# The last two eighths of the second feed-forward matrix taken together, and filler matmuls in planned gaps of TensorE

## The chip, the core and the metric

The kernel runs on one core of a Trainium2 chip. The metric is the device time of one execution in microseconds (us). TensorE (PE) multiplies matrices; VectorE (DVE), ScalarE (ACT) and GpSimd (POOL) do the elementwise work; SyncE (SP) issues the DMAs. TensorE's clock has two levels in this profile: a granted share of 1.0 is 2.4 GHz, of 0.5 is 1.2 GHz.

## What is computed

Two trunk layers run over 640 tokens: 128 prompt tokens and 512 sample tokens, which share all weights. From the reference, cut to the part that matters here:

```python
def trunk_layer(h, mod, lp, init, pos):
    sh1, sc1, g1, sh2, sc2, g2 = jnp.split(mod, 6, axis=-1)
    y, states = mixing_block(layer_norm(h) * (1.0 + sc1) + sh1, lp, init, pos)
    h = layer_norm(DEEPNORM_ALPHA * h + g1 * y, lp['ln1_g'], lp['ln1_b'])
    u = layer_norm(h) * (1.0 + sc2) + sh2
    f = jnp.square(jax.nn.relu(u @ lp['w_ff1'])) @ lp['w_ff2']
    h = layer_norm(DEEPNORM_ALPHA * h + g2 * f, lp['ln2_g'], lp['ln2_b'])
    return h, states
```

The model width is 1024, the hidden width of the feed-forward part 4096. `mixing_block` holds an input projection, four recurrent mixers (mLSTM, gated DeltaNet, retention, RWKV-7), and an output projection `w_out`.

## The kernel before, in words

**Tiles.** The 640 tokens are five tiles of 128: the group GA = tiles 0, 1, 2 and the group GB = tiles 3, 4. Matmuls run in fp32r on pairs: each operand is split into a high part (`wh`, `uh`, `hid` high) and a low rest (`wl`, `ul`), and a product is three matmuls. A weight block of 512 KB is loaded by SP into `wr`, cast by ACT (sometimes DVE) into `wh`, and the rest `wl` is formed by POOL or DVE (`split`). There are three `wr` buffers and two each of `wh` and `wl`. Six more buffers of the pool `pnz` are shared: they hold the hidden activations of an eighth, and some weights that are split early ("spare").

**Stages of a layer.** First the mixers: input projections (`pj`), scans, inverses (`lv`), head outputs (`pt` transposes of `osum`). Then `w_out` (`pwo`) and its layer norms (`wout_mm`, `wout_ln`), transposition into features for the feed-forward part (`put`, tiles `v`), and the feed-forward part in eighths of 512 hidden columns, counted by `hb`: `ff1(hb)` makes `hid` (four weight blocks, matmuls into `pj`), `ff2(hb)` multiplies with rows of `w_ff2` into banks `pff`, for two column halves of 512. Eighths 0 to 6 do `ff2` for all five tiles, four blocks of 30 matmuls, and add into `acc` (`add_first`, `add_mid`). Eighth 7 does `ff2` for GA first, four blocks of 18 matmuls, and then for GB, four blocks of 12, with `add_last`: scale by the gate (`fft`) and add to `acc`. Before that, `acc` is scaled and the residual `xr` is added to it. `final_ln` follows for GA beside the matmuls of GB, and then for GB; in layer 0 the result is normed once more and transposed (`put`) into the features `uh`, `ul` of layer 1, GA's 24 transposes first, then GB's 16.

**The modulation of layer 1** (`mod_chunk_v`, twelve chunks of four weight blocks, on ACT, DVE and POOL with a short `pmt` product on PE) is spread over layer 0's eighths: `next_mods(MB[0])` beside `ff1`, `next_mods(MB[1])` beside `ff2`.

**What sets the order.** Nothing is issued as it is written. Every operation is recorded as a node, and `Plan.schedule` runs a list scheduler over all of them: it has a cost for each instruction, a priority from the code's order and the longest path, room in the buffer pools, and a model of TensorE's clock (`hist`, `recent`, `cols`: matmul columns of the last few us). Its result is one fixed order for each engine, and each engine executes its own in that order. All instructions come out of one line (`emit`), so the profile names them all L743; they are told apart by their tiles.

## Time and profile before

| | |
|---|---|
| time of three runs | 2376.15 us median (2375.57 to 2382.08) |
| time of the profiled execution | 2374.3 us |
| its span, first to last instruction | 2372.5 us |
| mean granted TensorE clock | 0.939 |
| busy share | PE 89%, DVE 65%, ACT 40%, POOL 33% |

A row of the page's first part gives an engine's busy time, its share of the span and its instructions. PEclk in the second part is the granted clock in tenths, over 40 equal slices of the span. A matmul's record overlaps the next, so a mean duration is longer than the time from one start to the next. A matmul of plain f32 leaves two records.

### The profile page before, as it was taken

How to read it: one execution, taken by the hardware profiler on the slowest of the kernel's cores; microseconds unless marked ns; L12 is line 12 of the kernel's file. 1: busy time of each engine (PE TensorE's matmuls, PEld its weight loads, DVE VectorE, ACT ScalarE, POOL GpSimd, SP SyncE). 2: the span in 40 equal slices, each digit the busy share in tenths (PEclk: the TensorE clock that was granted, in tenths of full speed). 3: DMA queues.
4: the chain of work that ended last, by engine and by line, in shares of the span. 5: the costliest groups of instructions: out<-in, count | busy, mean ns of one | idle time of the engine just before them, and what ended most of it. 6: DMA issues, size and time to landing. Idle time of an engine off the chain costs nothing.

```text
span 2372.5 us, 42057 instructions
## 1 busy us (share of the span) xinstructions
PE 2113.5 (89%) x16510; PEld 1850.1 (78%) x16510; DVE 1544.2 (65%) x3245; ACT 949.9 (40%) x2018; POOL 774.0 (33%) x696
## 2 busy tenths in 40 slices
PE   5999989898786999999969989799897699999996
PEld 2887768787666888888947888689786589999995
DVE  5577767686679566667695768578785933333357
ACT  3444243343245544444344453343341443333332
POOL 2241323433246343335372325225361710000023
PEclk8999999999797999999977999899898899999998
DMA  8132442636343444444531222314353412222242
GB/s 265 28 73 73 112 101 74 171 91 176 127 139 118 141 134 134 134 133 138 158 116 37 64 43 69 71 54 99 91 149 129 141 61 72 80 72 80 72 160 89
DMA packets 317450, 253.12 MB, mean 107 GB/s; under 512 B 91100, under 2 KB 240828, under 8 KB 317252
## 3 DMA queue, kind: packets, MB, share of 16 engines
q1 hardware_dynamic: 317252, 250.43, 36.6%
q8 instruction: 130, 2.13, 0.4%
q14 instruction: 68, 0.56, 0.1%
HBM read 226.14 MB, written 24.24 MB: 106 GB/s over the span
## 4 chain that ended last, share of the span: by engine, by line
PE 57%; DVE 19%; DMA 9%; POOL 5%; issue 4%; ACT 3%; SPq 2%; DVEq 0%; POOLq 0%; ACTq 0%
PE pj L743 25%; PE pff L743 17%; DMA wr<-in_w_mod 3%; PE pwo L743 2%; SPq L743 2%; PE lv L743 2%; PE poo L743 2%; DVE xn L743 2%; DMA wr<-in_w_in 2%; DVE osum L743 1%; DVE lnrs L743 1%; DVE lnst L743 1%; DMA gh<-wscr 1%; DVE etmp L743 1%; DVE acc L743 1%
## 5 line engine op out<-in xcount | busy, mean ns | idle before, releaser
L743 ACT CAST wh<-wr 128x1024 fp32r<-128x1024 f32 x231 | 241.9, 1048 | 512.7 <-PE pff L743 225.0
L743 PE MATMUL pff<-wh,hid 128*128 128x512 f32 x1280 | 398.1, 393 | 0.0
L743 POOL TENSOR_TENSOR wl<-wr,wh 128x1024 fp32r<-128x1024 f32 x90 | 221.9, 2468 | 367.0 <-ACT wh L743 340.6
L743 DVE TENSOR_TENSOR wl<-wr,wh 128x1024 fp32r<-128x1024 f32 x144 | 188.8, 1311 | 214.0 <-ACT wh L743 213.7
L743 PE MATMUL pj<-uh,wl 128*128 128x256 f32 (+1 forms) x1056 | 309.3, 335 | 3.5 <-POOL wl L743 3.5
L743 PE MATMUL pj<-ul,wh 128*128 128x256 f32 (+1 forms) x1056 | 309.1, 335 | 0.0
L743 PE MATMUL pj<-uh,wh 128*128 128x384 f32 (+1 forms) x1056 | 306.1, 334 | 2.8 <-DVE dec L743 1.4
L743 PE MATMUL pj<-vh,wl 128*128 128x384 f32 (+1 forms) x1024 | 287.9, 312 | 1.8 <-POOL wl L743 1.1
L743 PE MATMUL pj<-vh,wh 128*128 128x384 f32 (+1 forms) x1024 | 285.3, 313 | 2.8 <-ACT wh L743 2.7
L743 PE MATMUL pj<-vl,wh 128*128 128x384 f32 (+1 forms) x1024 | 284.7, 312 | 0.0
L743 PEld LDWEIGHTS pff<-wh,hid 128*128 128x128 f32 x1280 | 239.7, 189 | 51.5 <-ACT wh L743 0.2
L743 PE MATMUL pff<-wl,hid 128*128 128x512 f32 x640 | 245.9, 397 | 10.3 <-POOL wl L743 10.0
L743 PEld LDWEIGHTS pj<-uh,wl 128*128 128x128 f32 x1056 | 193.4, 195 | 20.8 <-issue 9.5
L743 PEld LDWEIGHTS pj<-uh,wh 128*128 128x128 f32 x1056 | 193.2, 196 | 18.3 <-issue 7.0
L743 PEld LDWEIGHTS pj<-ul,wh 128*128 128x128 f32 x1056 | 194.2, 196 | 13.3 <-issue 8.7
L743 PEld LDWEIGHTS pj<-vh,wh 128*128 128x128 f32 x1024 | 186.5, 190 | 8.4 <-ACT wh L743 4.2
L743 PEld LDWEIGHTS pj<-vh,wl 128*128 128x128 f32 x1024 | 185.6, 190 | 4.7 <-POOL wl L743 1.5
L743 PEld LDWEIGHTS pj<-vl,wh 128*128 128x128 f32 x1024 | 186.0, 190 | 2.6 <-issue 1.4
L743 POOL TENSOR_TENSOR mac<-mac,mtm 128x512 f32<-128x512 f32 x77 | 114.1, 1482 | 177.4 <-ACT mtm L743 167.2
L743 DVE TENSOR_TENSOR hid<-sqr,hid 128x256 fp32r<-128x256 f32 (+1 forms) x125 | 73.0, 586 | 136.9 <-ACT hid L743 136.3
L743 POOL TENSOR_TENSOR acc<-acc,bc 128x512 f32<-128x512 f32 x16 | 26.8, 1693 | 387.8 <-DMA xr<-x1d 363.4
L743 PEld LDWEIGHTS pff<-wl,hid 128*128 128x128 f32 x640 | 119.2, 189 | 35.9 <-POOL wl L743 12.6
(499 smaller groups left out, 4139.8 us busy)
## 6 DMA issues: line engine op xcount, KB each, us to landing
wr<-in_w_ff SPq DMA_DIRECT2D x136, 512.0 KB
wr<-in_w_mod SPq DMA_DIRECT2D x96, 512.0 KB
wr<-in_w_in SPq DMA_DIRECT2D x66, 512.0 KB
wr<-in_w_out SPq DMA_DIRECT2D x32, 512.0 KB
dq<-rscr SPq DMA_DIRECT2D x20, 256.0 KB
dec<-rscr SPq DMA_DIRECT2D x16, 320.0 KB
x1d<-x SPq DMA_DIRECT2D x20, 256.0 KB
xr<-x1d SPq DMA_DIRECT2D x20, 256.0 KB
```

What stands on the lines that cost most here:

```text
L743: fn(*[res(v) for v in a], **{k_: res(v) for k_, v in k.items()})
```

## The change

It does four things.

1. `ff2` for eighth 6 is no longer done apart. `ff1(6)` and `ff1(7)` run in a row, and `ff2` then takes both at once, eight blocks of 18 matmuls for GA and then eight of 12 for GB. The hidden activations of eighth 6 stand in eight slots of the general pool.
2. Spare buffers take the early weights of three projections (`SPA = (6, 7, 8)`) and not of one.
3. Layer 1's modulation takes 6 and 2 steps in each of six eighths, before 5 and 2 in each of seven.
4. Stretches of the code are marked as zones (`thin`, `zone`): from the features `y` through `w_out` to the features `v`, and from GB's `ff2` through the final norm to the next layer's features, in both layers, and the first features at the start. Where the planner has no ready matmul for PE inside a zone, and its count of recent columns is under 1.3 of its mark, it puts in a filler: a 128x128 f32 matmul of the identity with 128 columns of constants into a fresh PSUM bank `warm`, which nothing reads.

Its core:

```diff
-    MB = (5,2,0,0,0,0)
-    SPA = (6,)
+    MB = (6,2,0,0,0,0)
+    SPA = (6, 7, 8)
...
+        FT, FT0, FB, FN = 1.3, 12.0, 2, 128
...
+                        if e == "PE" and (q is None or q is early) and now > FT0 and recent - part < FT * 3100 and any(a <= floor < b for a, b in self.zones) and caps[self.bank] > FB:
+                            nd, x = filler(now)
+                            d = nd.dur + (SW if nd.mode != mode else 0.0)
...
+    plan.warm = lambda n: (ident, cst[:, 0:n])
+    plan.warm_fn = lambda *a: nc.tensor.matmul(*a, start=True, stop=True)
...
-                hd = pnz.tile([128, 2, TOK], F32R, tag="nz", name=f"hid_{uid[0]}")
-                hi, lo = hd[:, 0, :], hd[:, 1, :]
+                if hb == 6:
+                    hi, lo = slot(TOK, "hid", F32R), slot(TOK, "hid", F32R)
+                else:
+                    hd = pnz.tile([128, 2, TOK], F32R, tag="nz", name=f"hid_{uid[0]}")
+                    hi, lo = hd[:, 0, :], hd[:, 1, :]
...
-                yield from acts_mm(hh, hl, tiles, (0, 1), lambda kk: I["w_ff2"][l, 512 * hb + 256 * kk:512 * hb + 256 * kk + 256, 512 * h_:512 * h_ + 512], banks)
+                yield from acts_mm(hh, hl, tiles, range(len(hid) // 2), lambda kk: I["w_ff2"][l, 512 * hb + 256 * kk:512 * hb + 256 * kk + 256, 512 * h_:512 * h_ + 512], banks)
...
-        for hb in range(7):
+        for hb in range(6):
...
+        run((ff1(6, hid), 8, "f"))
         run((ff1(7, hid), 8, "f"))
...
-        run((ff2(7, hid, GA, add_last), 6))
-        run((final_ln(GA), 3), (ff2(7, hid, GB, add_last), 6), (next_mods(MB[2]), 4))
+        run((ff2(6, hid, GA, add_last), 6))
+        with thin():
+            run((final_ln(GA), 3), (ff2(6, hid, GB, add_last), 6), (next_mods(MB[2]), 4))
```

The multiplications are the same, 240 `pff` matmuls for the two eighths of a layer. The weight blocks of eighth 6 are now loaded and split twice, once for GA and once for GB: four blocks more in each layer, 80 DMAs of 128x2x512 where there were 72. Ten `add_mid` per layer fall away. There are 163 fillers: 2 at the start; in layer 0, 17 ahead of `pwo` and 38 from the last `pwo` into the feed-forward part; 25 at the boundary of the layers; in layer 1, 16 ahead of `pwo` and 32 after it; and in the last stage 9 among the matmuls and 24 behind the last one.

Since the planner runs over everything at once, the order moves elsewhere too. With buffer numbers left out and set side by side, 8230 of some 12,900 PE instructions keep their place relative to each other, and the mixers of both layers are among what moved.

At the boundary of the layers, PE's queue before has GB's last matmuls and behind them the transposes of GA (`xn` are normed rows, `pff` banks of GB):

```order
L743 MATMUL pff_12618<-wh_12625,hid_12345 128x512
L743 MATMUL pff_12608<-wh_12625,hid_12416 128x512
L743 MATMUL pff_12618<-wh_12625,hid_12416 128x512
L743 MATMUL pff_12618<-wl_12650,hid_12416 128x512
L743 MATMUL pff_12618<-wh_12625,hid_12416 128x512
L743 MATMUL put_12710<-cst,xn_12702 128x128
L743 MATMUL put_12712<-cst,xn_12702 128x128
```

In the change, the first transposes stand inside GB's matmuls, behind 52 of the 96:

```order
L810 MATMUL warm_12760<-cst 128x128
L810 MATMUL warm_12764<-cst 128x128
L775 MATMUL pff_12704<-wl_12734,hid_11829 128x512
L775 MATMUL pff_12715<-wl_12734,hid_11829 128x512
L775 MATMUL put_12776<-cst,xn_12748 128x128
L775 MATMUL pff_12704<-wh_12699,hid_11838 128x512
L775 MATMUL pff_12715<-wh_12699,hid_11838 128x512
L775 MATMUL put_12786<-cst,xn_12748 128x128
L775 MATMUL pff_12704<-wh_12699,hid_11904 128x512
```

So `put` was behind all of GB's matmuls, and now 44 of them are queued behind the first `put`; 34 stand behind the eighth, and 11 behind the ninth. Between GA's transposes and GB's first, PE has 47 matmuls of the next projections (`pj`, `pgj`) before and 81 in the change.

In layer 1, ahead of the bulk of `pwo`, PE's queue before is this (`pt` transposes the last head output, `yh` is a feature of it after a trip through HBM):

```order
L743 MATMUL poo_19827<-Rd_18948,dec_17952 128x64
L743 MATMUL pt_3315_19867<-cst,osum_19720 128x128
L743 MATMUL pt_3316_19869<-cst,osum_19720 128x128 x4
L743 MATMUL pwo_19199<-wh_19490,yh_19881 128x512
L743 MATMUL pwo_19199<-wl_19559,yh_19881 128x512
```

and in the change:

```order
L775 MATMUL pt_3321_20039<-cst,osum_19920 128x128
L775 MATMUL pt_3322_20041<-cst,osum_19920 128x128 x4
L810 MATMUL warm_20051<-cst 128x128
L810 MATMUL warm_20053<-cst 128x128
L810 MATMUL warm_20055<-cst 128x128
```

16 fillers follow the five transposes there, all ahead of the first `pwo` that needs the last head.

## Rows read from the trace of the kernel before

**Rows 1.** The page's first and second part: busy time, granted clock by slice.

```profile
PE 2113.5 (89%) x16510; PEld 1850.1 (78%) x16510; DVE 1544.2 (65%) x3245; ACT 949.9 (40%) x2018; POOL 774.0 (33%) x696
PEclk8999999999797999999977999899898899999998
```

**Rows 2.** Busy time by stage, with its column line: mixers, feed-forward, boundary, end.

```profile
core 0: us, PE busy (x) PEld busy (x) DVE busy (x) ACT busy (x) POOL busy (x), PEclk, DMA share, GB/s
55.00:640.00 585.00, 534.81 (x5427) 462.55 (x5426) 414.80 (x1128) 227.46 (x584) 195.61 (x191) 0.94 0.39 103
754.00:1174.00 420.00, 411.97 (x2467) 370.49 (x2466) 270.01 (x298) 203.69 (x350) 154.79 (x97) 1.00 0.46 140
1196.00:1256.00 60.00, 34.73 (x144) 27.13 (x143) 53.51 (x87) 27.28 (x56) 45.38 (x47) 0.69 0.35 107
1256.00:1802.00 546.00, 496.92 (x5173) 445.23 (x5171) 394.16 (x1097) 218.31 (x563) 204.11 (x203) 0.94 0.32 80
1911.00:2316.00 405.00, 405.00 (x2299) 370.33 (x2299) 151.01 (x194) 146.11 (x251) 14.72 (x10) 1.00 0.27 85
2339.00:2373.00 34.00, 11.05 (x38) 7.65 (x36) 29.35 (x43) 6.77 (x8) 20.00 (x19) 0.73 0.21 77
```

**Rows 3.** PE's timeline at the boundary: start, duration, operation, [idle before, releaser].

```profile
1198.58 0.50 PE L743 MATMUL pff<-wl,hid 128*128 128x512 f32 x1 [0.45 <-POOL wl L743]
1209.18 0.80 PE L743 MATMUL pff<-wl,hid 128*128 128x512 f32 x1 [3.59 <-POOL wl L743]
1216.47 1.11 PE L743 MATMUL put<-cst,xn 128*128 128x128 f32 x4 [2.65 <-ACT xn L743]
1231.88 3.03 PE L743 MATMUL put<-cst,xn 128*128 128x128 f32 x13 [7.47 <-ACT xn L743]
1242.76 0.33 PE L743 MATMUL pj<-ul,wh 128*128 128x384 f32 x1
1242.93 0.33 PE L743 MATMUL pj<-uh,wl 128*128 128x384 f32 x1
1245.38 0.48 PE L743 MATMUL put<-cst,xn 128*128 128x128 f32 x1 [2.12 <-ACT xn L743]
```

**Rows 4.** PE's timeline, GB's part of the last eighth in layer 1.

```profile
2335.77 0.39 PE L743 MATMUL pff<-wh,hid 128*128 128x512 f32 x1
2336.00 0.39 PE L743 MATMUL pff<-wl,hid 128*128 128x512 f32 x1
2338.98 0.85 PE L743 MATMUL pff<-wh,hid 128*128 128x512 f32 x3
2340.28 0.50 PE L743 MATMUL pff<-wl,hid 128*128 128x512 f32 x1 [0.45 <-POOL wl L743]
2344.25 0.51 PE L743 MATMUL pff<-wl,hid 128*128 128x512 f32 x1 [0.95 <-POOL wl L743]
2350.94 0.55 PE L743 MATMUL pff<-wl,hid 128*128 128x512 f32 x1 [3.64 <-POOL wl L743]
2354.69 0.40 PE L743 MATMUL pff<-wh,hid 128*128 128x512 f32 x1
```

**Rows 5.** DVE's timeline at the end: the last bank's evacuation.

```profile
2358.53 0.68 DVE L743 TENSOR_TENSOR fft<-pff,bc 128x512 f32<-128x512 f32 x1
```

**Rows 6.** Groups by line: the two ways to form `wl`.

```profile
L743 POOL TENSOR_TENSOR wl<-wr,wh 128x1024 fp32r<-128x1024 f32 x90 | 221.9, 2468 | 367.0 <-ACT wh L743 340.6
L743 DVE TENSOR_TENSOR wl<-wr,wh 128x1024 fp32r<-128x1024 f32 x144 | 188.8, 1311 | 214.0 <-ACT wh L743 213.7
```

**Rows 7.** Nine stretches at the low clock inside the zones, summed by the same view as rows 2.

```profile
sum 122.80, PE 55.17 PEld 44.99 DVE 86.35 ACT 45.67 POOL 71.62; mean PE 6.13 PEld 5.00 DVE 9.59 ACT 5.07 POOL 7.96
```

**Rows 8.** Low stretches in which PE works without a break: two of `pwo`, then the sum of seven.

```profile
655.30:658.20 2.90, 2.83 (x7) 2.09 (x8) 0.84 (x2) 0.00 (x0) 0.00 (x0) 0.50 0.15 55
1817.30:1822.20 4.90, 4.84 (x11) 3.65 (x12) 0.83 (x2) 0.59 (x1) 0.00 (x0) 0.50 0.07 25
sum 23.20, PE 23.08 PEld 19.78 DVE 14.92 ACT 12.70 POOL 10.46; mean PE 3.30 PEld 2.83 DVE 2.13 ACT 1.81 POOL 1.49
```

**Rows 9.** PE's timeline around the gaps ahead of `pwo`, and a plain f32 matmul by form.

```profile
655.37 0.79 PE L743 MATMUL pwo<-wh,yh 128*128 128x512 f32 x1 [6.27 <-DVE yh L743]
1817.36 0.80 PE L743 MATMUL pwo<-wh,yh 128*128 128x512 f32 x1 [6.40 <-DVE yh L743]
L743 PE MATMUL pqs<-Yd,cvo 128*128 128x128 f32 x64 | 13.0, 302 | 0.2 <-DVE dtm L743 0.2
```

More of the change, by code (lines that the diff above doesn't have):

```diff
@@ L215, in __init__ @@
     def __init__(self):
-        self.nodes, self.tiles = [], []
+        self.nodes, self.tiles, self.zones = [], [], []
         self.HY = 1.0
@@ L484, in schedule @@
         HM = 1.2
+        FT, FT0, FB, FN = 1.3, 12.0, 2, 128
+        self.nfill = 0
         HG = 1.0
@@ L556, in schedule, with filler @@
         RES = 1
+        def filler(now):
+            x = self.warm_tile().tile
+            caps[x.key] -= 1
+            x.seq = x.at = x.end_seq = floor
+            load[x.key][floor] += 1
+            x.alloc = True
+            nd = Node()
+            nd.eng, nd.nm, nd.idx, nd.tiles, nd.preds, nd.succs, nd.grp = "PE", "matmul", len(N) + len(out), [x], [], [], None
+            nd.a, nd.k, nd.fn = (x.view()[:, 0:FN],) + self.warm(FN), {}, self.warm_fn
+            nd.mem, nd.act, nd.mode = [("matmul", nd.fn, nd.a, nd.k)], self.activity("matmul", nd.a[0], nd.a), self.pe_mode(nd.a)
+            nd.dur = self.pe_time(nd.mem)
+            return nd, x
         def eligible(nd, t):
@@ L826, in bankB, with thin, warm_tile @@
         return psA.tile([128, 512], F32, tag="a", name=f"{name}_{uid[0]}")
+    @contextmanager
+    def thin():
+        a = len(plan.nodes)
+        yield
+        plan.zones.append((a, len(plan.nodes)))
+    def warm_tile():
+        uid[0] += 1
+        return psA.tile([128, 512], F32, tag="a", name=f"warm_{uid[0]}")
+    plan.warm_tile = warm_tile
+    plan.bank = (id(psA), "a")
     def mm(out, lhsT, rhs, start=True, stop=True):
@@ L1431, in hybrid_step @@
     dma(out=mskt, in_=I["masks"])
-    run((to_features(0, 0, xn0, feats, FGA + FGB), 24))
+    with thin():
+        run((to_features(0, 0, xn0, feats, FGA + FGB), 24))
     for l in range(layers):
@@ L2272, in hybrid_step @@
         run((n3, 30), (ret_scan(1, C_[1], R_), 20, "f"), (mod_some(40), 40))
+        zone = len(plan.nodes)
         yhl = new_features("y")
@@ L2312, in hybrid_step @@
         run((wout_mm(GA), 10))
-        run((wout_ln(GA), 3), (wout_mm(GB), 10))
-        u2 = new_features("v")
-        run((to_features(l, 2, xn, u2, FGA), 16))
-        if l + 1 < layers:
-            load_params(l + 1)
-            nmod = mod_gen(l + 1, (0, 2, 1, 3) + tuple(range(4, NMX)))
-        run((wout_ln(GB), 2))
-        run((to_features(l, 2, xn, u2, FGB), 8))
+        plan.zones.append((zone, len(plan.nodes)))
+        with thin():
+            run((wout_ln(GA), 3), (wout_mm(GB), 10))
+            u2 = new_features("v")
+            run((to_features(l, 2, xn, u2, FGA), 16))
+            if l + 1 < layers:
+                load_params(l + 1)
+                nmod = mod_gen(l + 1, (0, 2, 1, 3) + tuple(range(4, NMX)))
+            run((wout_ln(GB), 2))
+            run((to_features(l, 2, xn, u2, FGB), 8))
         u2h, u2l = [f[0] for f in u2], [f[1] for f in u2]
```

31 lines of the change are left out of this document (23 added, 8 removed).

## The prediction

> **What bounds the kernel now.** I read the page's busy shares and clock first, then busy time by stage, then PE's timeline where PE stands still. PE is busy 89% of the span, no other engine over 65%, and PEclk dips in some slices [rows 1]. The stages differ [rows 2]. The feed-forward part of layer 1 is PE alone: 405.0 of 405 us. In layer 0 the same part has 8.0 us of PE idle in 420, beside the modulation of the next layer. The mixers leave PE idle for 50.2 us of 585 in layer 0 and 49.1 of 546 in layer 1. At the boundary of the layers, 1196 to 1256, PE works 34.7 of 60 us while DVE works 53.5, at a mean clock of 0.69: there the norms on DVE set the pace, and PE waits for `xn` with 2.65 us, 7.47 us and later 2.12 us of idle ahead of transposes [rows 3]. In the last 34 us DVE works 29.4 and PE 11.1 [rows 2]. So PE work that moves into the boundary is hidden, and a shorter stay at the low clock pays only where PE has work queued.
>
> **Part 1: eighth 6 joins eighth 7.** Matmuls of `pff` start 0.23 us apart at full clock [rows 4]. GB's 48 matmuls of eighth 6 (48 x 0.23 = 11.0 us) leave the place ahead of GA's end, where PE is busy without a break, and join GB's own 48 behind it.
>
> At the boundary they fall into 60 - 34.7 = 25.3 us of PE idle. GA's end comes 11.0 us earlier, and the DVE-bound stretch behind it stays as long as it was, but for four more weight blocks. One costs DVE 1.31 us or POOL 2.47 us [rows 6]; all on DVE would be 5.2 us, all on POOL 9.9 us of the 14.6 us that POOL is idle there [rows 2], or none. I take +4 (0 to +10), near the DVE price, since DVE has only 6.5 us free. The ten `add_mid` that fall away lay beside PE's work in eighth 6, so I count nothing for them. The spare buffers let 81 projection matmuls stand ahead of GB's transposes and not 47; they start 0.17 us apart [rows 3], so up to 34 x 0.17 = 5.8 us of work moves into the idle stretch that begins at 1243. What moves must wait for its weights, and those come when the hidden tiles are freed, so I take -3 (0 to -5.8). Sum at the boundary: -11.0 + 4 - 3 = **-10** (-16.8 to -1).
>
> At the kernel's end there is no next layer to hide in. Before, the stretch from 2339.0 to the end is 33.5 us, and 11.0 us of GB's eighth 6 lie ahead of it: 44.5. After, GB has 96 x 0.23 = 22.1 us of matmuls, in blocks of 12, 2.8 us each, which is less than the weights take: the three changes of block shown cost 0.45, 0.95 and 3.64 us, all waits for `wl` [rows 4]. Seven such changes cost 3.2 us by the least, 11.8 us by the mean of 1.68; I take 8. The tail behind the last matmul (2355.1) is 17.4 us now, but DVE had a backlog there: it came to the last bank only at 2358.53 [rows 5], 14.0 us from the end. With GA's norms done beside the longer GB part the tail is between these; I take 15. 22.1 + 8 + 15 = 45.1 against 44.5: **+0.6** (-5.2 to +6.8).
>
> **Part 2: fillers.** In the zones the clock is low for 122.8 us, but PE works only 55.2 us of that [rows 7]; the idle rest loses nothing by a slow clock. Work at half clock takes twice as long, so nothing over 55.2 / 2 = 27.6 us can come back. Much of it is transposes that wait for norms anyway; in the seven stretches with PE at work without a break it is 23.1 us, worth 11.5 [rows 8]. The surest are the two `pwo` starts: 7 matmuls in 2.83 us and 11 in 4.84 [rows 8], which at 0.23 us are 1.6 and 2.5: 3.5 us together. In front of them stand gaps of 6.27 and 6.40 us [rows 9], and 17 and 16 fillers. A filler is like `pqs`: 64 records in 13.0 us, two records a matmul [rows 9], so 0.41 us, or half of that where they overlap more: 3.4 to 7.0 us for 17. That fits the gap. But nothing spaces them out: PE takes them as soon as it reaches them, so in a gap longer than planned they are spent at its start. After the last `pwo` 19 and 23 fillers stand in gaps of some 13 us, and I expect little from these. I take 3.5 for `pwo` and 1.5 for the rest: **-5**. The bounds are -27.6, and +14 if both clusters ahead of `pwo` run at the low clock throughout (33 x 0.82 = 27.1 us against 12.7 us of gaps). The 24 behind the last matmul lie beside a tail of 15 us.
>
> The clock has the levels 0.5 and 1.0 in these rows, and half of the low time is idle. The Trainium skill (TensorE: Matmul & The Clock Gate, Terms) puts the penalty at the whole throttled time multiplied by one minus the granted share. That would be an estimated 122.8 x 0.5 = 61.4 us in the zones, and the rows contradict it with 27.6 as the most.
>
> **Part 3: modulation.** Eight steps in each of six eighths, not seven in each of seven. If the 8.0 us of PE idle grow with the density, 8.0 x (8/7 - 1) = **+1** (0 to +3). The last chunk's `pmt` moves behind `ff2` of GA; what it may wait for is inside that range.
>
> **Part 4: the re-planned mixers.** The planner's order changed there, with no aim that I can read from it. PE idle there is 50.2 + 49.1 = 99.3 us [rows 2]. I take **0**, with -10 to +10: a tenth of it either way.
>
> **Sum.** -10 + 0.6 - 5 + 1 + 0 = -13.4. The profiled execution takes 2374.3 us, so 2360.9 there; it lies 1.85 us under the median of the three runs, so **2363 us** against 2376.15. Its own range is 2352 to 2371.
>
> **The rivals.** A change of 0.3% is 7.1 us, about what a measurement of this kernel can tell from none: faster is under 2369.0, slower over 2383.3.
>
> *A new wait takes the gain.* PE's queue now has GB's matmuls behind GA's transposes: the first stands behind 52 matmuls, 12.0 us after GA's end, with 44 behind it. Before, the first transpose started at 1216.47, 20.5 us into the stretch [rows 3]. If the norm is not faster, PE waits 8.5 us with GB's matmuls behind it, and GB's norms start late. For it: DVE is full there. Against: GB's evacuations now come later, so DVE has less between GA's steps. With the end at its upper bound: 2363 + 8.5 + 6.2 = 2378, no change.
>
> *The fillers do nothing*, being spent at the start of each gap: 2363 + 5 = 2368.
>
> *Slower: the mixers' new order.* If PE's idle time in the mixers grows by a quarter of 99.3 us, the time is 2363 + 25 = 2388. It is slower from a growth of 13.4 + 7.1 = 20.5 us, a fifth. For it: nearly all of the kernel's waits on chains and DMAs lie there, and the order is made of estimates. Against: the mixers' work is unchanged.
>
> *The clock stays up everywhere:* 27.6 in place of 5 gives 2363 - 22.6 = 2340. Against it: fillers stand in seven clusters, and gaps of 13 us are longer than 19 x 0.41 = 7.8 us.
>
> *The whole low time comes back*, half of 122.8 us: 2363 - 56 = 2307. Rows 7 speak against it. This is the skill's rule above.
>
> **How the numbers follow.** Forecast 0.45 (0.40 of it faster, 0.05 same); fillers without effect 0.14 (0.08 and 0.06); a new wait 0.16 (same); mixers 0.17 (slower); clock up everywhere 0.06 (faster); the whole low time 0.02 (faster). Faster 0.56, same 0.27, slower 0.17. The range is 2344 to 2388: it leaves out the upper half of the mixers' case, half of the clock's and the last, some 0.14.
>
> **What would show it.** Right: from GA's last `pff` to the first projection of layer 1 some 38 us as before with 96 GB matmuls inside; the stretch between the layers with PE idle near 10 us and not 25; `pwo` starting at clock 1.0 in both layers; the feed-forward part of layer 1 still without PE idle; about 45 us from GA's end to the last instruction. Wrong: PE idle ahead of `put` with GB's matmuls behind it; waits for `wl` over 12 us in the last GB part; fillers still running when `yh` is ready; or a sum of PE idle in the mixers far from 99 us, which would make every other term small beside it.

## The result, and the profile after

The changed kernel takes 2402.5 us (median of 4, 2398.29 to 2407.96) against 2379.11 us for the kernel before beside it (4, 2375.57 to 2385.31): 1.0086 times as long, 95% interval 1.006 to 1.0112. The forecast was 2363 with a range to 2388, so both the direction and the range were missed. The profiled execution takes 2399.31 us, its span 2397.5 us, 25.0 us over that of before.

The page of the changed kernel, first and second part, against [rows 1]:

```profile
PE 2157.2 (90%) x16836; PEld 1897.9 (79%) x16836; DVE 1548.8 (65%) x3263; ACT 947.7 (40%) x2013; POOL 781.6 (33%) x679
PEclk7999999999798999999998999899897999999999
```

PE has 43.7 us more busy time, nearly all of it the 163 fillers (some 42 us); the other engines have about as much as before. The mean clock is higher, 0.946 against 0.939; the dip at the boundary (two slices of 7) is down to one slice of 8, and that in the last slice is gone, while the mixers' dips lie elsewhere. By the signs that the change aims at it should be faster.

Busy time by stage in the changed kernel, cut where PE's own stages end: the mixers of layer 0, its eighths 0 to 5, from there to the last `put` of the boundary, the mixers of layer 1, its eighths 0 to 5, the joined eighths, the tail:

```profile
core 0: us, PE busy (x) PEld busy (x) DVE busy (x) ACT busy (x) POOL busy (x), PEclk, DMA share, GB/s
59.00:651.00 592.00, 535.35 (x5391) 465.44 (x5390) 404.92 (x1126) 218.15 (x574) 194.12 (x190) 0.92 0.37 100
767.00:1125.00 358.00, 337.61 (x1977) 299.69 (x1977) 233.70 (x262) 168.91 (x293) 148.72 (x90) 0.98 0.45 135
1125.00:1283.00 158.00, 143.42 (x815) 127.22 (x814) 111.01 (x155) 73.45 (x131) 70.56 (x53) 0.97 0.45 137
1283.00:1838.00 555.00, 493.62 (x5148) 444.86 (x5147) 397.52 (x1110) 218.79 (x564) 195.67 (x190) 0.93 0.32 79
1942.00:2264.00 322.00, 322.00 (x1807) 292.26 (x1806) 114.41 (x151) 114.92 (x199) 1.87 (x3) 1.00 0.26 76
2264.00:2384.00 120.00, 115.27 (x641) 102.52 (x640) 77.32 (x90) 48.13 (x76) 33.75 (x21) 1.00 0.42 136
2384.00:2397.00 13.00, 5.32 (x48) 5.13 (x46) 10.03 (x17) 1.63 (x2) 4.82 (x6) 0.83 0.22 81
```

The kernel before by the same cuts where [rows 2] has others: eighths 0 to 5 of layer 0, from there to the last `put`, and the last two eighths of layer 1:

```profile
753.00:1093.00 340.00, 332.21 (x1969) 296.74 (x1968) 215.73 (x248) 169.29 (x291) 118.70 (x76) 1.00 0.45 134
1093.00:1255.00 162.00, 136.49 (x749) 119.90 (x748) 123.76 (x162) 70.75 (x130) 85.73 (x69) 0.89 0.45 138
2236.00:2355.00 119.00, 113.96 (x626) 102.22 (x624) 71.54 (x91) 43.81 (x71) 29.42 (x20) 0.99 0.36 115
```

The boundary went from 162 to 158 us and from a clock of 0.89 to 0.97. But the eighths of layer 0 grew from 340 to 358 us, and the mixers from 584 to 592 and from 547 to 555.

**Lost time.** Stages that end at a certain instruction also change when other work crosses that instruction. So the runs below are compared by what PE loses in each stage: its idle time, the time of the fillers, and half of its other busy time at the granted clock 0.5. All three are summed from PE's instructions and the clock's records; where a filler overlaps a matmul its time can be counted in two ways, which differ by up to 7 us in a kernel's sum; the figures lie between. The span less this sum lies between 2017.7 and 2022.1 us in 17 of the 20 kernels profiled (2025.1 to 2029.2 in three), so the rest is nearly the same in all, and the lost time accounts for most of the differences.

| us lost | start | mixers, layer 0 + 1 | `pwo` to `put`, both layers | eighths 0-5, layer 0 | boundary | from eighth 6 of layer 1 | sum |
|---|---|---|---|---|---|---|---|
| before | 32.2 | 79.2 + 78.4 | 94.9 | 8.4 | 34.3 | 24.2 | 351.7 |
| after | 36.5 | 99.3 + 90.3 | 80.2 | 27.4 | 24.5 | 20.3 | 378.5 |
| difference | +4.3 | +32.0 | -14.7 | +19.0 | -9.8 | -3.9 | +26.8 |

Less 1.8 us of other work, that is the 25.0 us of the span. (The rest of layer 1's feed-forward part loses 0.3 us before and none after.) Three stages gained 28 us; the mixers, layer 0's eighths and the start took 55.

PE's timeline of the changed kernel at the boundary, every idle time of 0.9 us and over from 1222 on, against [rows 3]:

```profile
1225.43 0.80 PE L775 MATMUL pff<-wl,hid 128*128 128x512 f32 x1 [3.72 <-POOL wl L775]
1230.92 0.50 PE L775 MATMUL pff<-wh,hid 128*128 128x512 f32 x1 [0.94 <-ACT wh L775]
1242.06 0.73 PE L775 MATMUL pff<-wl,hid 128*128 128x512 f32 x2 [0.95 <-POOL wl L775]
1248.77 0.50 PE L775 MATMUL pff<-wh,hid 128*128 128x512 f32 x1 [1.09 <-ACT wh L775]
1251.49 0.55 PE L775 MATMUL put<-cst,xn 128*128 128x128 f32 x3 [1.77 <-DVE xn L775]
1257.51 2.50 PE L810 MATMUL warm<-cst 128*128 128x128 f32 x20 [1.46 <-DVE fft L775]
1278.60 0.48 PE L775 MATMUL put<-cst,xn 128*128 128x128 f32 x1 [4.51 <-ACT xn L775]
```

The 7.47 us ahead of GA's transposes are gone: GB's matmuls and 13 fillers stand there, and 12 more fillers behind them. What is left is waits for weights, the longest 3.72 us, and for `xn`, the longest 4.51 us for GB's.

PE's timeline around the two `pwo` starts of the changed kernel, against [rows 9]:

```profile
660.01 3.96 PE L810 MATMUL warm<-cst 128*128 128x128 f32 x34
669.40 0.80 PE L775 MATMUL pwo<-wh,yh 128*128 128x512 f32 x1 [5.42 <-DVE yh L775]
...
1845.32 1.30 PE L775 MATMUL pt<-cst,osum 128*128 128x128 f32 x5 [7.77 <-DVE osum L775]
1846.41 5.42 PE L810 MATMUL warm<-cst 128*128 128x128 f32 x32
1853.09 0.50 PE L775 MATMUL pwo<-wh,yh 128*128 128x512 f32 x1 [1.26 <-DVE yh L775]
```

And five stretches of it, with the columns of busy time by stage: the fillers in the first gap and the matmuls behind it, the first half of the fillers in the second gap and the matmuls behind it, and a stretch in eighth 5 of layer 0:

```profile
660.00:663.90 3.90, 3.90 (x36) 3.78 (x34) 1.21 (x3) 0.00 (x0) 0.00 (x0) 1.00 0.62 217
669.40:672.30 2.90, 2.90 (x7) 2.34 (x8) 0.80 (x1) 0.00 (x0) 0.00 (x0) 0.50 0.09 34
1846.40:1849.90 3.50, 3.50 (x19) 3.50 (x18) 0.69 (x1) 0.00 (x0) 0.00 (x0) 0.50 0.25 94
1853.10:1858.00 4.90, 4.90 (x22) 4.04 (x23) 2.20 (x3) 1.05 (x1) 0.00 (x0) 1.00 0.07 24
1092.20:1095.60 3.40, 3.40 (x10) 3.21 (x11) 2.80 (x2) 1.04 (x3) 3.32 (x3) 0.50 0.38 133
```

In layer 0 the 17 fillers run at 1.00 and are spent in 3.96 us, 5.42 us of idle follow, and `pwo` starts at 0.50 with 7 matmuls, as in [rows 8]. In layer 1 the clock had fallen during the 7.77 us ahead of `pt`; the fillers run at 0.50 at first and at 1.00 from 1849.94 on. They end 1.26 us ahead of `yh`, and `pwo` starts at 1.00: 22 matmuls in 4.9 us, where [rows 8] had 11. The last stretch is new: matmuls of an eighth at half clock, behind a wait of 2.44 us for `wh`.

### The profile page after: what moved, and what is told of

Same layout as the page of the kernel before. It is cut to its first block, busy times and chain, and to the rows that moved or that the text cites. A ratio compares the mean times of both kernels' runs of the same rounds, so it can differ in the third digit from the quotient of the medians.

```text
span 2397.5 us, 42735 instructions
## 1 busy us (share of the span) xinstructions
PE 2157.2 (90%) x16836; PEld 1897.9 (79%) x16836; DVE 1548.8 (65%) x3263; ACT 947.7 (40%) x2013; POOL 781.6 (33%) x679
## 5 line engine op out<-in xcount | busy, mean ns | idle before, releaser
L775 ACT CAST wh<-wr 128x1024 fp32r<-128x1024 f32 x237 | 248.1, 1048 | 486.4 <-PE pff L775 219.8
L775 POOL TENSOR_TENSOR wl<-wr,wh 128x1024 fp32r<-128x1024 f32 x100 | 248.3, 2486 | 357.8 <-ACT wh L775 352.3
L775 PE MATMUL pj<-uh,wl 128*128 128x384 f32 (+1 forms) x1056 | 315.1, 338 | 12.7 <-POOL dec L775 7.1
L775 PE MATMUL pj<-ul,wh 128*128 128x384 f32 (+1 forms) x1056 | 313.6, 338 | 2.6 <-issue 2.6
L775 PE MATMUL pj<-vh,wh 128*128 128x256 f32 (+1 forms) x1024 | 284.3, 311 | 1.2 <-ACT wh L775 1.0
L775 PEld LDWEIGHTS pj<-uh,wh 128*128 128x128 f32 x1056 | 196.3, 198 | 22.9 <-issue 11.5
L775 PEld LDWEIGHTS pj<-ul,wh 128*128 128x128 f32 x1056 | 197.2, 198 | 13.1 <-issue 8.0
L775 PEld LDWEIGHTS pj<-vh,wh 128*128 128x128 f32 x1024 | 186.0, 190 | 4.5 <-ACT wh L775 1.9
L775 POOL TENSOR_TENSOR mac<-mac,mtm 128x512 f32<-128x512 f32 x72 | 107.3, 1490 | 176.8 <-ACT mtm L775 158.5
L775 DVE TENSOR_TENSOR hid<-sqr,hid 128x256 fp32r<-128x256 f32 (+1 forms) x125 | 79.7, 640 | 113.2 <-ACT hid L775 113.0
L775 PEld LDWEIGHTS pff<-wl,hid 128*128 128x128 f32 x640 | 119.4, 190 | 36.2 <-POOL wl L775 11.3
L775 DVE SCALAR_TENSOR_TENSOR mac<-wr,cc,mac 128x512 f32<-128x512 f32 x84 | 97.8, 1165 | 50.8 <-DMA wr<-in_w_mod 34.6
```

The lines of the kernel that those rows point to most:

```text
L775: fn(*[res(v) for v in a], **{k_: res(v) for k_, v in k.items()})
```

## Experiments: undoing parts of the change

The theory was that the denser modulation and the mixers' new order had cost the time, and the boundary and the fillers had gained; the rival, that the joined eighths or the fillers were at fault.

**a_mod5**, the changed kernel with the modulation at seven steps an eighth; eighth 6's seven stand beside the two joined first matrices:

```diff
-    MB = (6,2,0,0,0,0)
+    MB = (5,2,0,0,0,0)
-        run((ff1(6, hid), 8, "f"))
-        run((ff1(7, hid), 8, "f"))
+        run((ff1(6, hid), 8, "f"), (next_mods(MB[0]), 3))
+        run((ff1(7, hid), 8, "f"), (next_mods(MB[1]), 1))
```

> The changed kernel with the modulation at its old density: 5 and 2 steps per eighth, the last 7 of them beside ff1 of eighths 6 and 7. Theory 1 (density): eight steps per eighth put more modulation weights ahead of the feed-forward weights in SP's queue and in the three wr buffers, so PE waits for wh and wl 13.9 us in layer 0's first six eighths where it waited 1.6 us, and then runs at the low clock. Then these eighths come back from 358 us to about 340 (end of the features v to the end of eighth 5), PE's waits for wh and wl there fall under 4 us, and the time falls by some 18 us. Rival (the order alone): the stalls come from the new plan whatever the density, and stay within 4 us of 358; the time stays within 7 us of the changed kernel.

Measured: 1.0042 times before (1.0025 to 1.006). Layer 0's eighths take 345.9 us and lose 16.3, against 358.0 and 27.4. PE's waits for `wh` and `wl` there (weight waits; those of 0.4 us and over are summed) are 4.1 us, where the changed kernel has 13.9. The time fell by 11 us, not by 18. But the boundary now loses 42.0 us, where the changed kernel loses 24.5 and before 34.3. So the steps cost where they stand, and here the joined eighths gained at the boundary only with the steps out of the way.

**a_nofill**, the changed kernel without fillers (`FB` at 99, a count of free banks that is never reached):

> The changed kernel without fillers (the bank condition is never met). Theory 2 (fillers pay a little): both starts of the bulk of pwo run at the low clock again, 1 and 2 us longer, the stretches from the last poo to the end of the features v together 2 to 6 us longer, the time 2 to 6 us more. Rival (fillers cost): those stretches get shorter, and the time is 3 us or more less. The order in the mixers moves too, since the planner's clock changes; if the mixers of either layer move by over 4 us although no filler stands in them, that is the order alone.

Measured: 1.0042 (1.0022 to 1.0062). In layer 1 the stages from the last `poo` to the end take 570.9 us, against 560.0 with fillers and 570.4 before. So the fillers give 11 us there, and yet the kernel without them is the faster one by its median of 2390.17 us (the profiled execution took 2399.03). Its layer-0 eighths lose 16.6 us, where the changed kernel loses 27.4, and its mixers 198.9. Outside the mixers it loses 179.8 us, against 188.9 with fillers. Fillers that gain where they stand, in a kernel that is slower with them: that needs a term outside the stages they stand in.

**a_spa6**, the changed kernel with `SPA = (6,)`:

> The changed kernel with one early projection in the spare buffers as before, not three. If three early projections pay at the boundary, PE has some 34 matmuls fewer ahead of GB's transposes and the stretch from the first pgj of layer 1 to its end of mixers is 2 to 5 us longer. If the spare buffers cost (they are also those of the solves of the mixers, which then start later), the mixers of both layers fall back towards 584 and 547 us, 8 us each, and the time falls by 10 to 16 us.

Measured: 1.0084 (1.0063 to 1.0105), lost time 383.4, boundary 21.7, eighths 28.4. Neither of its two expectations came: the spare buffers explain none of the loss.

## Experiments: one part alone on the kernel before

**b_mod6**, before with `MB = (6,2,0,0,0,0)`:

> The kernel before with 6 and 2 steps per eighth, nothing else: the modulation is then done after six of the seven eighths. Theory 1 (density): PE's waits for wh and wl in the first six eighths grow from 1.6 us to over 8 us, with low-clock stretches behind them, eighth 6 without modulation gains 3 us, and the time is 8 to 16 us more than the kernel before. Rival (the order alone): under 4 us either way.

Measured: 1.0071 (1.0047 to 1.0096). The eighths lose 16.2 us against 8.4, weight waits 9.6 against 1.6; the boundary loses 33.7, as before. The larger part is in the mixers of layer 1: 107.9 us lost against 78.4, although nothing of them was changed (the profiled execution is the slowest of six, 11.4 us over their median).

**b_join**, before with the two eighths joined, the modulation spread as in a_mod5, no fillers, `SPA = (6,)`:

> The kernel before with the two last eighths joined and nothing else: no fillers, one early projection, modulation at 5 and 2 steps in all eight eighths. Theory (joining itself pays at the boundary): from the end of eighth 5 to the end of layer 1's features the time falls from 162.6 us by 5 to 10 in spite of the same modulation, the layer-1 end stays within 3 us of 136.3, and the total is 4 to 12 us under the kernel before. Rival (modulation beside ff1(6) and ff1(7) takes it): that stretch is 8 us longer or more, as in the changed kernel at 5 steps (173.4), and the total is the same or more.

Measured: 1.0102 (1.0075 to 1.013). The boundary loses 45.8 us against 34.3, the end 20.7 against 24.2. That is what its rival said.

**b_fill**, before with the fillers alone (`thin`, `zone` and `filler` as in the change, the eighths apart, `MB` and `SPA` as before):

> The kernel before with fillers and nothing else; eighths apart, modulation and spare buffers as before. Theory (fillers pay in their zones): in layer 1 the stretches of pwo, of the features v and of the feed-forward part are together 6 to 9 us shorter than 69.4 + 38.7 + 326.0, as the changed kernel against its twin without fillers; layer 0's are 0 to 4 us shorter; the rest of the kernel moves only by the order. Total 3 to 12 us less than before. Rival (the new plan that fillers bring costs more elsewhere): the zones shorten but the mixers or layer 0's eighths lengthen, and the total is the same or more.

Measured: 0.9934 (0.991 to 0.9958), 2370.03 us. Its median is below those of both kernels. `pwo` to `put` loses 79.6 us against 94.9, the boundary 28.2 against 34.3.

## Experiments: another order for the same work

The mixers' lost time had moved in every kernel, also where the edit did not touch them. So two of the planner's margins were shifted by a hair, in the kernel before: `SLK`, its tolerance in picking the engine of an operation, and `MG`, how long it holds back a matmul that has just become ready.

**b_slk** and **b_mg**:

```diff
-        SLK=0.2
+        SLK=0.21
```

```diff
-        MG = 0.3
+        MG = 0.31
```

> The kernel before, with one number of the planner moved that has no meaning here: the slack by which an operation prefers its first engine is 0.21 us, not 0.20. The work is the same, only the order and some choices of engine move. Theory (the order alone moves the time): the total lands 5 to 20 us off the kernel before, either way but more likely above, most of it in the mixers. Rival: within 4 us, and then the mixers' growth in the changed kernel needs another cause than a new order.

> The kernel before with another such number: PE's operations wait 0.31 us in the planner after they are ready, not 0.30. The same two theories: 5 to 20 us off, most of it in the mixers, or within 4 us.

Measured: 1.01 (1.0077 to 1.0122) and 1.0022 (1.0004 to 1.0041). The first is 24.6 us off, more than the 20 expected, the second 5.2. The shift of `SLK` by 0.01 us costs as much as the whole change. Then the same two shifts in the changed kernel and in the one with fillers alone:

> The changed kernel with the planner's constant SLK at 0.21 for 0.2: nothing of what is computed or of the change's parts differs, only the order that the planner writes. Theory A (the change's parts cost time wherever the order falls): eighths 0 to 5 of layer 0 take 350 to 360 us again with 8 to 15 us of weight waits, against 339.8 before, and the time is 2398 to 2410. Rival B (the order drawn for the mixers decides the sign, the parts are worth little): the mixers' two stages differ from those of the changed kernel by 10 us or more, and the time can lie anywhere from 2380 to 2410.

> The changed kernel with the planner's constant MG at 0.31 for 0.3, again only another order. Theory A: eighths 0 to 5 of layer 0 take 350 to 360 us with 8 to 15 us of weight waits; 2398 to 2410. Rival B: the time lies anywhere from 2380 to 2410, following PE's idle time and the time at the low clock in the mixers.

> The kernel with the fillers alone, SLK at 0.21 for 0.2. If the fillers' 11 us in layer 1's stages outside the mixer are their own, those stages (last poo to the end) take 560 to 564 us here too, against 570.4 before, and the time is 2385 to 2398, some 11 us under the kernel before with the same constant (2405.74). If the fillers' gain was a lucky order as well, those stages take 567 us or more, and the time is over 2400.

> The kernel with the fillers alone, MG at 0.31 for 0.3. If the fillers' gain is their own: 560 to 564 us from the last poo of layer 1 to the end, and 2368 to 2382, some 11 us under the kernel before with the same constant (2386.25). If not: 567 us or more there, and 2385 or more.

| ratio to before | margins as they were | `SLK` 0.21 | `MG` 0.31 | mean |
|---|---|---|---|---|
| before | 1 | 1.0100 | 1.0022 | 1.004 |
| fillers alone | 0.9934 | 0.9991 | 0.9964 | 0.996 |
| the change | 1.0086 | 0.9945 (2364.76 us) | 1.0068 | 1.003 |

The change with `SLK` at 0.21 is faster than before, 0.9926 to 0.9965, with every part of the change in it. The lost time says where these differ:

| us lost | mixers | all other stages | eighths 0-5 | boundary |
|---|---|---|---|---|
| before, three orders | 157.6, 188.3, 178.9 | 194.1, 197.2, 187.1 | 8.4, 12.2, 10.6 | 34.3, 34.1, 33.4 |
| fillers alone | 168.2, 167.7, 169.5 | 181.8, 182.1, 182.1 | 16.4, 13.3, 13.5 | 28.2, 28.8, 28.1 |
| the change | 189.6, 161.0, 177.0 | 188.9, 186.4, 186.0 | 27.4, 24.8, 25.8 | 24.5, 22.9, 25.1 |

Outside the mixers a stage of one kernel repeats within 4 us in its three orders, but for `pwo` to `put` in layer 1 (40.3 to 47.7 us before, 34.7 to 39.6 with the fillers alone). The mixers go from 157.6 to 198.9 us over all 20 kernels, mean 177, and the kernel before with its own margins is the lowest of all. Both theories of a_slk and a_mg held in part: the eighths cost 355.8 and 357.0 us again, as expected of the parts, and the time still followed the mixers. Three times came out below what was expected: a_slk's 2364.76 us lies under both theories, and the fillers alone take 2374.51 and 2365.35 us, though their stages came as expected.

What PE waits for in the mixers of layer 1, the longest of the sums: before, the changed kernel, and the changed kernel with `SLK` at 0.21 (us in total, times, longest):

```profile
PE lv L743 <- issue: 16.3, 6, 8.0
PE pbv L743 <- DVE wmk L743: 6.7, 2, 6.0
```

```profile
PE lv L775 <- issue: 14.8, 4, 8.5
PE pst L775 <- DMA zo<-in_state_rwkv: 7.1, 1, 7.1
PE pj L775 <- POOL dec L775: 7.1, 1, 7.1
```

```profile
PE pbv L775 <- DVE wmk L775: 6.3, 3, 5.1
PE psb L775 <- DVE cst L775: 5.4, 1, 5.4
```

Each order has its own few long waits, on a chain, a transfer or a decay factor. Why the planner's order brings them is not shown. The same stage with `SLK` at 0.21 takes 523 us, where the row of the changed kernel above has 555:

```profile
1286.00:1809.00 523.00, 482.75 (x5153) 434.68 (x5151) 401.53 (x1106) 213.93 (x558) 204.65 (x200) 0.96 0.33 82
```

20.7 us of idle less (the stage's sums are 60.9 and 40.2), and about as many matmuls in 10.9 us less of busy time, at a mean clock of 0.96 and not 0.93.

Not all of the mixers' scatter is the order. Up to eighth 0 of layer 0, a_mod5 has the instructions of the changed kernel in the same order on all five queues, and its mixers of layer 0 take 583 us, not 592:

```profile
58.00:641.00 583.00, 524.81 (x5392) 454.62 (x5391) 404.31 (x1127) 217.89 (x574) 194.04 (x191) 0.94 0.38 101
```

Idle time is nearly the same (58.2 and 56.6 us); PE's busy time is 10.5 us apart, at 0.94 against 0.92. So one profile of the mixers is good to some 9 us, and differences of a few us in that column mean nothing. Two kernels of the next sections, m43 and a_half, have that order there too. The four lose 99.3 (the changed kernel), 87.7 (a_mod5), 97.0 and 95.4 us in layer 0's mixers, while b_mod6, which has the order of the kernel before there, loses 80.0 and before 79.2. So some 15 us in layer 0 belong to the order and not to the execution.

## Experiments: joined eighths beside the modulation, and fillers beside them

**m5_slk** and **m5_mg** are a_mod5 with the two shifted margins; **m43** is a_mod5 with four and three steps in place of five and two (and the three beside eighth 7's matrix recorded at a denser pace, 3 for 1); **an_slk** is a_nofill with `SLK` at 0.21.

> The changed kernel with the modulation left at seven steps an eighth, five beside eighth 6's first matrix and two beside eighth 7's, and SLK at 0.21. Lost time below means PE idle, filler time and half of PE's busy time at the low clock. Theory J (eighths joined beside the modulation cost time in themselves): 42 to 46 us are lost from the end of eighth 5 to the last put, as with the same split and the other order (42.0), against 28.1 to 28.8 with the fillers alone; weight waits of eighths 0 to 5 under 6 us; the time is some 12 us over the fillers alone with this constant (2374.5), so 2380 to 2392. Rival: the 42.0 was one order's; 28 to 34 us are lost there, and the time is 2360 to 2374.

> The same with MG at 0.31 in place of SLK. Theory J: 42 to 46 us lost from the end of eighth 5 to the last put, and 2370 to 2384 (the fillers alone with this constant: 2365.4). Rival: 28 to 34 us, and 2352 to 2366.

> The same with the planner's constants as they were, and four steps beside eighth 6's first matrix and three beside eighth 7's. If the waits ahead of pmt in the joined first matrices (2.99, 5.88 and 3.9, 5.6 us with five and two) come from the five steps that stand beside 24 us of PE work, they fall by half, and 35 to 38 us are lost from the end of eighth 5 to the last put; if they come from the joining alone, 42 us again. The time: 2380 to 2395 by the mixers' order.

> The changed kernel without fillers (their bound on free banks set out of reach) and with SLK at 0.21. If the fillers are worth in the changed kernel what they are worth alone (17 us in the mean of three orders), it takes some 2375 to 2390, against 2364.76 with fillers and this constant; if the time of that kernel was the mixers' order alone, 2365 or less is as likely as 2400. In layer 1's stages behind the mixer 567 to 570 us, against 560.7 with fillers.

Measured, as ratio to before: m5_slk 0.9987 (0.9965 to 1.0009), m5_mg 1.0142 (1.0113 to 1.0171), m43 1.0039 (1.002 to 1.0059), an_slk 1.0025 (0.9998 to 1.0053). At the boundary m5_slk loses 41.0 us and m5_mg 44.4, so the 42.0 of a_mod5 was no accident of one order, and its rival falls. The times did not follow: m5_slk's 2379.14 us is just under its range, and m5_mg's 2416.34 us is 32 us over it, with 194.0 us lost in the mixers. m43 loses 37.9, the upper end of what was expected if density is the cause. The first long wait of `pmt` stays (3.8 us in m5_slk, 3.9 in m43), and the second is shorter, but not halved; first m5_slk, then m43:

```profile
1155.99 1.08 PE L775 MATMUL pmt<-mac,cst 128*32 128x128 f32 x16 [5.62 <-DVE mac L775]
```

```profile
1162.43 0.64 PE L775 MATMUL pmt<-mac,cst 128*32 128x128 f32 x16 [3.55 <-DVE mac L775]
```

So the density beside the joined matrices is a part of it, and the rest stays unexplained. By the ratios (0.9945 and 1.0025) the change with this margin is 0.8% faster with its fillers than without, as expected; with the first margins it was 0.4% slower with them. The stages from the last `poo` of layer 1 to the end take 568.3 us without fillers and 560.7 with; f_slk and f_mg have 561.1 and 561.5 there, as expected. That gain holds in layer 1. Over all stages outside the mixers it does not: fillers are worth 8.5 us in the changed kernel with this margin (194.9 less 186.4), and cost 9.1 with the first margins (179.8 and 188.9). In both, layer 0's eighths lose more with fillers: 24.8 against 16.7 us, and 27.4 against 16.6.

## Experiments: why eight steps cost so much

In the changed kernel 13.9 of PE's 20.4 us idle in eighths 0 to 5 are weight waits, of which the kernel before has 1.6. They come with the eight steps: 5.3 to 14.8 us in the seven kernels that have them, leaving out the two below, and 1.6 to 4.7 in the eleven with seven steps. Groups of PE's instructions there, `pff<-wh` and `pj<-vh,wl`, before and then after (count | busy, mean ns | idle before them):

```profile
L743 PE MATMUL pff<-wh,hid 128*128 128x512 f32 x480 | 148.4, 391 | 0.0
L743 PE MATMUL pj<-vh,wl 128*128 128x256 f32 (+1 forms) x360 | 101.8, 309 | 0.7 <-DVE wl L743 0.7
```

```profile
L775 PE MATMUL pff<-wh,hid 128*128 128x512 f32 x480 | 152.1, 398 | 7.8 <-ACT wh L775 7.8
L775 PE MATMUL pj<-vh,wl 128*128 128x256 f32 (+1 forms) x355 | 100.5, 310 | 5.2 <-POOL wl L775 3.7 <-DVE wl L775 1.4
```

ACT's timeline of the changed kernel ahead of the first such wait, with two later waits of ACT, and PE's behind the first:

```profile
783.48 0.72 ACT L775 ACTIVATE mtm<-wr,cc 128x512 f32<-128x512 f32 x1 [4.50 <-DMA wr<-in_w_mod]
784.11 0.36 ACT L775 ACTIVATE relu<-pj 128x256 f32<-128x256 f32 x1
784.38 1.03 ACT L775 CAST wh<-wr 128x1024 fp32r<-128x1024 f32 x1
...
795.72 0.73 ACT L775 ACTIVATE mtm<-wr,cc 128x512 f32<-128x512 f32 x1 [7.91 <-DMA wr<-in_w_mod]
...
1089.87 1.33 ACT L775 ACTIVATE mtm<-wr,cc 128x512 f32<-128x512 f32 x2 [3.26 <-DMA wr<-in_w_mod]
```

```profile
785.46 2.50 PE L775 MATMUL pff<-wh,hid 128*128 128x512 f32 x5 [2.66 <-ACT wh L775]
```

A modulation step (`mtm`) stands at the head of ACT's queue and waits 4.50 us for its weights. The `wh` that PE needs is queued behind it. Modulation and feed-forward share three `wr` buffers and one queue of loads. Two kernels tell what is late.

**a_half**, the changed kernel whose modulation of layer 1 loads half of each block:

```diff
-            raw = wraw(I["w_mod"][l, 256 * kk:256 * kk + 256, 512 * n:512 * n + 512], 2, 512)
+            if l:
...
+                dma(out=raw[:, 0:512], in_=I["w_mod"][l, 256 * kk:256 * kk + 128, 512 * n:512 * n + 512])
...
-                rw = raw[:, 512 * e:512 * e + 512]
+                rw = raw[:, 0 if l else 512 * e:512 if l else 512 * e + 512]
```

**a_nwr4**, with one more buffer:

```diff
-    NSL, NFL = 31, 0
-    NWR, NWH = 3, 2
+    NSL, NFL = 30, 0
+    NWR, NWH = 4, 2
```

> The changed kernel in which layer 1's modulation loads half of each of its weight blocks (128x512 in place of 128x2x512) and uses that half twice: the bytes are halved, the steps, their operations and their number stay; layer 1's modulation comes out different. In the changed kernel ACT waits up to 7.9 us for such a load with `mtm` at the head of its queue, and `wh` for the feed-forward stands behind it. Theory D (the denser steps cost time because their loads come late): the weight waits of eighths 0 to 5 fall from 13.9 us to under 6, the eighths from 358.0 to 340 to 348 us. Rival O (the operations of the added steps on ACT, DVE and POOL are what delays wh and wl): weight waits stay at 10 us or more, and 352 to 360 us. The time follows the mixers' order: 2375 to 2405.

> The changed kernel with four buffers for raw weight blocks in place of three, and 30 general slots in place of 31 to make room. Theory D, if the loads come late for want of a free buffer: weight waits of eighths 0 to 5 under 6 us, 340 to 348 us. If the transfers themselves are what is late, or the operations (rival O): weight waits of 10 us or more, 352 to 360 us. The time: 2370 to 2410 by the mixers' order; the slot taken away may add to PE's idle time there.

Measured: a_half takes 0.9969 times before (0.9946 to 0.9993). Its eighths take 341.7 us and lose 14.7, the weight waits are 0.0 us, with all the added operations in place. So the operations alone are not the cause, and the loads are. What is left there is near the 13.3 to 16.4 of the fillers alone. The stage in a_half, and the group of `pff<-wh` in it:

```profile
766.00:1107.00 341.00, 331.08 (x1971) 295.97 (x1964) 223.86 (x251) 170.24 (x293) 138.36 (x84) 0.99 0.37 108
```

```profile
L775 PE MATMUL pff<-wh,hid 128*128 128x512 f32 x479 | 147.9, 391 | 0.2
```

ACT's waits for modulation weights in these eighths, before, after and in a_half (us in total, times, longest):

```profile
ACT mtm L743 <- DMA wr<-in_w_mod: 52.2, 25, 3.8
```

```profile
ACT mtm L775 <- DMA wr<-in_w_mod: 59.5, 24, 7.9
```

```profile
ACT mtm L775 <- DMA wr<-in_w_mod: 38.3, 22, 4.4
```

The sum hardly grows with the change, the longest wait doubles. But its length does not tell which wait reaches PE. The longest, 7.91 us, delays no matmul. Behind one of 4.50 us and one of 5.72 (845.30) PE waits 2.66 and 2.68 us, and behind one of only 3.26 us (1089.87) it waits 2.44, since the `wh` that it needs next is queued there. a_nwr4 takes 342.5 us for its eighths, with 2.7 us of weight waits, at the full number of bytes: a fourth buffer does nearly as much as half the bytes. Part of that is moved, since the order put one chunk's `pmt` behind eighth 5 and the boundary loses 31.1 us; both stages together lose 43.1 us, against 51.9 after and 42.7 before. As a whole it takes 1.0057 (1.0033 to 1.0082), the mixers of layer 0 losing 101.9 us and idle for 72.8 of it, with the slot less.

## Why the prediction was wrong, step by step

**What bounds the kernel.** This held. Layer 1's eighths are PE alone, 322.00 of 322 us. At the boundary GA's norms set the pace: the first `put` starts 21.5 us after GA's end, as before (1214.82 to 1236.36, and 1194.92 to 1216.47). The rival *a new wait takes the gain* did not come: the 52 matmuls ahead of the first `put` were given 12.0 us, but with waits for weights, `pmt` and seven fillers among them they take as long as the norm.

**Part 4, the re-planned mixers, 0 within 10: this is the step that failed.** They lost 32.0 us more, 20.1 in layer 0 and 11.9 in layer 1; 18.7 of it is idle time and 13.3 half clock. The row of 99.3 us idle was read as a property of the work, with a tenth of it as scatter. It is a property of one order, and the lowest of 20: the other 19 kernels lose 177.7 us there in the mean, this one 157.6. In the mean of three orders the mixers lose 174.9 us before and 175.9 after, so no net cost of the change is shown there. That it has none is not shown either. In layer 0 the three kernels with the change lose 99.3, 101.1 and 104.9 us, the three before 79.2, 91.8 and 73.8; in layer 1 it is the other way, 90.3, 59.9 and 72.1 against 78.4, 96.5 and 105.1. Whether that is the change or the draw of orders, three of each can't tell.

17 us of the kernel before, then, were its own, and edits that make the planner start again gave them up on average. Part of them belongs to one profiled execution: it took 2374.3 us, and the six medians of this kernel that stand beside the other runs lie between 2378.16 and 2382.41. The case that the text priced at 2388, *the mixers' new order*, is the one that came, and it had a chance of 0.17. Its threshold, a growth of 20.5 us, was passed with clock and idle together; idle alone grew by 18.7.

**Part 3, the modulation, +1 (0 to +3): the second step that failed.** The eighths lost +19.0 in this order and +15.6 in the mean of three (26.0 less 10.4). The mechanism was wrong: the 8.0 us of idle were scaled with the density, as if each step cost its share. Most of them were waits of `pmt`, 5.6 us, and these hardly grew, to 6.3. What grew was another thing: the added loads came late in front of a `wh` that PE needed, 13.9 us of weight waits where there were 1.6. Behind two of these waits and one of `pmt` matmuls ran at half clock, 6.3 us lost by that. Not all of the 15.6 is the steps': the fillers alone have 14.4 in these eighths, and the eight steps without fillers 16.2 to 16.7 (b_mod6, a_nofill, an_slk). So the steps cost some 6 us without fillers and 11.6 with them, and why fillers make them dearer is open.

**Part 1, the boundary, -10 (-16.8 to -1):** -9.8 in the changed kernel, -9.7 in the mean of three, and -8.3 without fillers (25.6 us lost in the mean of a_nofill and an_slk, 33.9 before). The size is right, but the sum counted the boundary as if the seven steps beside eighth 6 were free. They were moved away by Part 3's edit, and with them left there the joined eighths lose 41.0 to 44.4 us, 7 to 10 us more than before (37.9 in m43). So joining and density have to be priced as one edit. With fillers the two together cost 4 us (-4.2 at the boundary, +11.6 in the eighths, -3.4 at the end, against the fillers alone); without fillers they give 3.6 (-8.3, +6.3 and -1.6). So no net worth of the joined eighths is shown. From GA's end to the first projection it takes 45.0 us, not the 38 of the text: 39.6 before, 11.0 us of matmuls and some 6 us of fillers more, and less idle time and half clock.

**Part 1, the end, +0.6 (-5.2 to +6.8):** the stretch after was sized well, with luck in its terms: GA's end to the last instruction was put at 45.1 = 22.1 + 8 + 15, and it is 44.40 = 22.1 + 8.7 + 13.6, but of the 8.7 us 4.6 are waits for `wh` and `wl`, some 2 are nine fillers, and 2 are not accounted for. The 44.5 before was read wrong. It starts at 2339.0 [rows 4], and GA's 72nd matmul ends at 2336.62; so it was 46.9, and the end gained 2.5 us. The stage agrees: 134.1 us against 136.3.

**Part 2, the fillers, -5 (-27.6 to +14):** right in sign where they stand alone. On the kernel before they are worth 10.8 us outside the mixers in the mean of three orders (192.8 less 182.0), twice the term; in the changed kernel 8.5 us with one margin and -9.1 with the other, the eighths taking back what the zones give. The steps were half right: in layer 0 the fillers are spent at the start of the gap and `pwo` starts at half clock, as the text feared, and in layer 1 it starts at full clock. Most of the gain is where little was expected. From `pwo` to `put` in layer 1 half clock cost 6.9 to 9.2 us in the three orders of before and costs 2.0 to 3.0 with the fillers alone, while idle and filler time together stay about as they were (36.2 and 35.5 us in the mean); the boundary gives 5.5. A filler takes 0.23 us at a granted clock of 1.00 (17 in 3.96 us) and 0.43 at 0.50 (the first eight of layer 1 in 3.4 us); the text took 0.41, or half of that.

The rule of the Trainium skill that the text weighed (TensorE: Matmul & The Clock Gate, Terms) puts what the low clock costs in the zones at an estimated 61.4 us. In the stages that hold them half clock cost 26.5 us before and 8.6 to 13.9 in the six kernels with fillers in the table of orders, so at most 18 us came back; the bound of 27.6 from the rows stands.

**The sum.** Outside the mixers the change is worth -5.7 us in the mean of three orders, where the text had -13.4. By stages: start +2.7, `pwo` to `put` -10.7, layer 0's eighths +15.6, boundary -9.7, end -3.4. The difference is Part 3, less what the zones and the end gave beyond their terms. By the means of three orders (1.003 and 1.004) the change makes no measurable difference. The terms' own bounds add up to -59.6 and +32.8 us, or 2317 to 2409; the range that was given, 2344 to 2388, is narrower than that, and the mixers' bound of 10 us was a guess with nothing measured behind it. The 1.0086 is the distance between a poor order of the one and a good order of the other.

Open: what in an order makes the mixers wait, and what makes the clock's dips fall differently in the same order, was not tried. Three orders leave the mean of each kernel uncertain by 0.2 to 0.4% (its standard error). So the 0.8% between the means of before and of the fillers alone is some two standard errors, and in the changed kernel the fillers gave 0.8% with one margin and -0.4% with the other: their gain is shown stage by stage, not for the whole.

## What to carry to other kernels

Where a planner writes the order, shift one of its margins by a hair, several times, before a change is priced or judged: the spread is the smallest difference that a single comparison can show, and the kernel at hand may stand at its lucky end. Judge parts by the stages that they touch, by idle time and time at half clock, which here repeated within a few us outside the mixers. And try a part with and without the others: the fillers gave 10.8 us alone and nothing sure beside the denser steps. A step that is hidden with a wait of its own in front (here `mtm`, where 7.91 us delayed nothing and 3.26 did) is not priced by its density: look for what is queued behind it, and for the buffer that its load needs.

## What the runs showed of the hardware

- The same instructions in the same order on all queues take 583 to 592 us in layer 0's mixers in four kernels, at a granted clock of 0.94 to 0.92, with about the same idle time (55.5 to 58.2 us).
- In layer 0's eighths of the changed kernel the clock fell from 1.00 to 0.50 at three single waits: for 6.8 us at one of 2.66 us (785.46), for 3.4 us each at one of 1.73 (897.58) and one of 2.44 (1092.19). It is not the wait's length alone: at one of 2.68 us (847.28) and one of 3.49 (1018.73) the clock stayed at 1.00. Before, it never fell there behind waits of up to 1.84 us.
- A plain f32 matmul of 128x128 with 128 columns leaves two records and takes 0.23 us from one to the next at a granted clock of 1.00, as long as one `pff` matmul of 512 columns (0.23 us, [rows 4]), and 0.43 us at 0.50.
